# Loop over further expert rounds placed behind the last expert, router logits in one product, and tokens placed ahead of their weights in a two-layer diffusion transformer with a mixture of experts

## The chip, the cores and the metric

One Trainium2 chip, one of its cores. The metric is the device time in microseconds of one execution; lower is better. The engines are called TensorE (PE; its weight loads are listed as PEld), VectorE (DVE), ScalarE (ACT), GpSimd (POOL) and SyncE (SP). SyncE computes nothing here; it issues DMA transfers. GpSimd issues some as well, through its own software queue (q0 in the listings; SyncE's is q1).

## The reference, cut to what matters

256 latent tokens and 256 context tokens of width 1024 pass two layers. Layer 0 mixes them by attention, layer 1 by an S5 state-space scan. Each layer ends with a mixture of 32 experts in 4 groups, of which every token uses two. In layer 1 only the latent tokens are needed after the mixer.

```python
def hierarchical_moe(h, w_group, b_group, w_router, b_router, w_gate, w_up, w_down):
    t = h.reshape(-1, D_MODEL)
    g_logits = (t @ w_group + b_group)
    g_idx = jnp.argmax(g_logits, axis=-1)
    g_w = jnp.max(jax.nn.softmax(g_logits, axis=-1), axis=-1, keepdims=True)
    e_logits = (t @ w_router + b_router).reshape(-1, MOE_GROUPS, MOE_EXPERTS_PER_GROUP)
    e_logits = jnp.einsum('tg,tge->te', one_hot(g_idx, MOE_GROUPS), e_logits)
    e_w, e_idx = lax.top_k(jax.nn.softmax(e_logits, axis=-1), MOE_TOP_K)
    e_w = e_w / jnp.sum(e_w, axis=-1, keepdims=True)
    expert = g_idx[:, None] * MOE_EXPERTS_PER_GROUP + e_idx
    combine = jnp.einsum('tk,tke->te', g_w * e_w, one_hot(expert, MOE_EXPERTS))
    for e in range(MOE_EXPERTS):
        hid = jax.nn.silu(t @ w_gate[e]) * (t @ w_up[e])
        y = y + combine[:, e:e + 1] * (hid @ w_down[e])
```

## The kernel before

The kernel is written against a tile framework with a manual schedule: the order of instructions on each engine is the order of the Python code, and generators (`prep`, `open`, `quad`, `turned` and others) are advanced by hand with `next` to interleave them. The program is straight-line code except for one loop, in `overflow`, which stands twice, once for each layer.

An expert holds 64 slots (`W`). A token's place in an expert is its rank among the tokens that chose it. If an expert has more than 64 tokens, further rounds are needed; `count` (L736) computes the number of rounds into `rounds`, and `overflow` (L1022) loads it into a register of every engine (L1026), copies the places (L1028, L1029) and runs a `For_i` loop (L1030) from round 1 to that number. With the inputs of this case there is one round, so the loop body runs zero times.

Layer 0 has four tiles of 128 tokens (`nt` = 4), layer 1 two. For each tile `prep` (L597) normalises the tokens, transposes them on TensorE (L626), forms the router logits (L633, a copy L636, a second product L647 with a selector, and the bias at L649), and `route` (L653) chooses the group and the two experts with some thirty small VectorE instructions, forms the ranks (L689) and the weights (L697 to L706). `place` (L710) builds a one-hot of the slot (L717) and, with a product (L718), writes the token number and its weight into the slot table `acc` in PSUM. The last tile advances `opening`, which contains `count`.

`experts` (L937) begins with `slots` (L720), which copies `acc` to SBUF, and then differs by layer:

- Layer 0 (`direct`): `pairs` (L728, four copies on GpSimd) and `indices` (L811) form row numbers, three `gather`s (L824, issued on GpSimd) fetch the token rows of experts 0 to 5 from a DRAM copy `td`, GpSimd issues the weights of expert 2, `overflow` stands, and `turned` (L828) transposes the first gathered rows (L835).
- Layer 1: `overflow` stands, then `pairs` and the one-hots for the next four experts. Rows are selected by products (`take`, L761) with split copies `parts` of the tokens (L642 on ScalarE, L643 on GpSimd).

Then 32 experts follow. For each, `hidden` (L841) does the gate and up products (L848), `down` (L864) the second product (L869) of the expert before. Every second expert, `places` and `split` scale the results (L897, L898; in layer 1's last pair L891), and `combine` (L907) adds them back to the tokens with products (L913). The last pair is combined in `last`, which in layer 0 also issues the first S5 loads (`s5.load(7)`, in the order v0 v1 v2 w0 k0 w1 v3; two more, w2 and v4, follow at the scan's first step) and in layer 1 the output transfers (L1903).

Weights are fetched by SyncE, three transfers of 1 MB for an expert, into a ring of slots: 11 in layer 0, 16 in layer 1. SyncE issues a transfer when the slot's last reader is done, and takes its instructions in order. Ahead of `experts`, layer 0 fetches two experts (`ahead(2)`), layer 1 five.

## Time and profile before

| | us |
|---|---|
| median of 3 runs | 1153.84 |
| lowest and highest | 1153.43, 1157.52 |
| the profiled execution, its own time | 1157.44 |
| its span, first to last instruction | 1155.7 |
| mean granted TensorE clock, of 2.4 GHz | 0.942 |
| TensorE busy | 987.2 (85%) |
| VectorE busy | 730.1 (63%) |
| ScalarE busy | 324.6 (28%) |
| GpSimd busy | 139.9 (12%) |

Times of instructions below are from the span's start. The first layer's experts begin at 403 us and end at about 720; the S5 scan runs from there to about 845; the second layer's experts run from 882 to the end. A granted clock of 0.50 is the lower of TensorE's two levels (1.2 GHz), 1.00 the upper one.

### The profile page before, as it was taken

What the parts mean: (1) busy time and instruction counts of PE and PEld (TensorE: products, weight loads), DVE (VectorE), ACT (ScalarE), POOL (GpSimd) and SP (SyncE); (2) the same over time, 40 slices, a digit from 0 to 9 for tenths busy, and PEclk for the clock granted to TensorE, in tenths of its full rate; (3) what the DMA queues carried; (4) which work ended last, traced back from release to release, by engine and by line L of the source; (5) the groups of instructions that cost most, each with busy time, mean ns of one, the idle gap of its engine ahead of it and who ended that gap; (6) DMA issues with size and microseconds to landing.
All of it is one profiled execution on the core that took longest, in us unless ns stands there. A gap on an engine that the chain in (4) does not pass through costs nothing. (4 is left out here: it accounts for less than half of the span.)

```text
span 1155.7 us, 17511 instructions
## 1 busy us (share of the span) xinstructions
PE 987.2 (85%) x6627; PEld 552.9 (48%) x6627; DVE 730.1 (63%) x1804; ACT 324.6 (28%) x704; POOL 139.9 (12%) x206
## 2 busy tenths in 40 slices
PE   2798889879998199999988977678977999999997
PEld 0443444444444055555544532365755555555553
DVE  7779888993445214455788987399974444534444
ACT  3422334343111032121221212693531211221210
POOL 2311121123111100000000002011421000000000
PEclk9899999989999589999998988889987999999999
DMA  9954854855994889999885886399975999999951
GB/s 298 353 178 137 287 197 151 276 198 174 386 407 143 332 317 409 385 403 354 329 333 205 321 323 158 90 227 327 393 283 232 355 382 383 377 378 380 384 200 37
DMA packets 88232, 331.75 MB, mean 287 GB/s; under 512 B 10040, under 2 KB 18968, under 8 KB 69712
## 3 DMA queue, kind: packets, MB, share of 16 engines
q1 hardware_dynamic: 68736, 290.05, 68.3%
q10 hardware_dynamic: 11424, 21.12, 5.2%
q0 software_dynamic: 7984, 19.42, 5.0%
q8 instruction: 54, 0.88, 0.3%
q14 instruction: 34, 0.28, 0.1%
HBM read 313.76 MB, written 20.99 MB: 290 GB/s over the span
## 5 line engine op out<-in xcount | busy, mean ns | idle before, releaser
L848 PE MATMUL gu<-ring,xq 128*64 128x256 f32 x1056 | 147.1, 394 | 4.6 <-DVE sl L853 2.3
L848 PE MATMUL gu<-more,xq 128*64 128x256 f32 x992 | 135.9, 386 | 0.0
L848 PEld LDWEIGHTS gu<-ring,xq 128*64 128x64 f32 x1056 | 83.3, 142 | 63.5 <-issue 28.4
L913 PE MATMUL co<-yh,oT 128*128 128x512 f32 x188 | 87.9, 468 | 24.6 <-DVE z L904 9.1
L848 PEld LDWEIGHTS gu<-more,xq 128*64 128x64 f32 x992 | 77.0, 138 | 53.4 <-issue 23.3
L352 PE MATMUL acc<-ring,uT 128*128 128x512 f32 x192 | 91.7, 609 | 2.9 <-ACT uT L328 2.9
L852 ACT ACTIVATE sl<-gu 64x256 f32<-64x256 f32 x64 | 24.1, 377 | 247.0 <-PE gu L848 247.0
L921 DVE TENSOR_TENSOR sum<-sum,co 128x512 f32<-128x512 f32 x92 | 59.5, 682 | 33.6 <-PE co L913 33.5
L913 PE MATMUL co<-yl,oT 128*128 128x512 f32 x188 | 78.4, 417 | 0.6 <-DVE yl L898 0.6
L853 DVE TENSOR_TENSOR sl<-gu,sl 64x256 f32<-64x256 f32 x64 | 27.3, 426 | 79.4 <-ACT sl L852 78.2
L861 DVE COPY hT<-ht 128x128 f32<-128x128 f32 x64 | 18.4, 287 | 87.5 <-PE ht L859 87.4
L869 PE MATMUL y<-ring,hT 128*64 128x512 f32 x272 | 68.8, 628 | 0.4 <-DVE hT L861 0.4
L913 PEld LDWEIGHTS co<-yh,oT 128*128 128x128 f32 x188 | 35.8, 191 | 59.1 <-issue 18.2
L869 PE MATMUL y<-more,hT 128*64 128x512 f32 x240 | 58.0, 604 | 0.4 <-DVE hT L861 0.4
L352 PEld LDWEIGHTS acc<-ring,uT 128*128 128x128 f32 x192 | 34.4, 193 | 36.5 <-issue 32.5
L142 PE MATMUL gv<-ring,cT 128*32 128x256 f32 x512 | 34.6, 412 | 18.0 <-DMA ring<-mod_w 18.0
L915 DVE TENSOR_TENSOR h<-h,co 128x512 f32<-128x512 f32 x64 | 41.1, 681 | 5.7 <-PE co L913 5.7
L821 POOL DMA_INDIRECT xg<-td,row x16 | 16.1, 1006 | 208.1 <-PE xt L835 206.3
L913 PEld LDWEIGHTS co<-yl,oT 128*128 128x128 f32 x188 | 36.5, 194 | 8.5 <-DVE yl L898 5.4
L835 PE MATMUL xt<-ident,xg 128*128 128x128 f32 x128 | 22.0, 300 | 20.6 <-issue 19.9
L407 ACT ACTIVATE pr<-sc,mx 128x256 f32<-128x256 f32 (+1 forms) x32 | 18.6, 580 | 74.5 <-DVE mx L406 74.5
L898 DVE SCALAR_TENSOR_TENSOR yl<-z,pt,yh 128x512 fp32r<-128x512 f32 x30 | 22.5, 751 | 25.8 <-ACT yh L897 25.8
(434 smaller groups left out, 1856.7 us busy)
## 6 DMA issues: line engine op xcount, KB each, us to landing
ring<-moe_w_down SPq DMA_DIRECT2D x34, 1024.0 KB, 9.8
ring<-moe_w_gate SPq DMA_DIRECT2D x33, 1024.0 KB, 7.6
ring<-moe_w_up SPq DMA_DIRECT2D x33, 1024.0 KB, 8.3
ring<-mod_w SPq DMA_DIRECT2D x32, 1024.0 KB, 8.5
more<-moe_w_gate SPq DMA_DIRECT2D x30, 1024.0 KB, 7.4
more<-moe_w_up SPq DMA_DIRECT2D x30, 1024.0 KB, 9.2
more<-moe_w_down SPq DMA_DIRECT2D x29, 1024.0 KB, 11.2
more<-mod_w SPq DMA_DIRECT2D x16, 1024.0 KB, 15.5
```

The lines of the kernel that those rows point to most:

```text
L142: nc.tensor.matmul(self.bank[i, b][32 * q:32 * q + 32, o:o + 256], self.cT[:, k, :], self.tiles[i, ch, k // 2][:, k % 2, 256 * q:256 * q + ...
L352: nc.tensor.matmul(acc, uT[:, k, 128 * t:128 * t + 128], wq[b][k // 4][:, k % 4, :], start=(k == 0), stop=(k == KT - 1))
L407: nc.scalar.activation(pr[:, 0:nk], s[:, 0:nk], AF.Exp, bias=mx[:, h, 0:1], accum_out=mx[:, h, 1:2])
L835: nc.tensor.transpose(p[:, 128 * i:128 * i + 128], self.xg[:, k % 3, 4 * b + i::KT], self.c.ident)
L848: nc.tensor.matmul(p[s:s + 64, 0:HID], xT[k], w[k // 4][:, k % 4, :], start=(k == 0), stop=(k == KT - 1), skip_group_check=True)
L852: nc.scalar.activation(sl, p[0:64, 0:HID], AF.Silu)
L853: nc.vector.tensor_tensor(sl, p[64:128, 0:HID], sl, op=OP.mult)
L869: self.c.nc.tensor.matmul(p[o:o + 64, :], hT[:, f, :], wd[f][:, 512 * n:512 * n + 512], start=(f == 0), stop=(f == 1), skip_group_check=True)
L898: nc.vector.scalar_tensor_tensor(lo, y, w, hi.bitcast(F32), op0=OP.mult, op1=OP.subtract)
L913: nc.tensor.matmul(p, oh[:, 128 * n:128 * n + 128], y, start=(i == 0), stop=(i + 1 == len(rows)))
L915: nc.vector.tensor_tensor(h, h, p, op=OP.add)
L921: nc.vector.tensor_tensor(a, a, p, op=OP.add)
```

## The change

- `overflow` leaves the head of `experts` and is called at the end of the loop over experts, behind the `split` of the last pair and ahead of `last`. In its body one tile is replaced by a part of another.
- The logits are one product: the transposed tokens are the weights, the router's 40 columns move. The copy, the selector product and one step of the generator go; the bias is added from PSUM.
- In `route`, the negated maxima and the three exponentials move behind the choice of experts. The token numbers are placed first, in columns 0 to 31 of `acc`, the weights later, in columns 32 to 63, with the same one-hots.
- In layer 0 a new `start`, called by the last tile's `route` between the two placings, computes the row numbers from `acc` directly and issues the three gathers and expert 2's weights. `pairs` and `slots` run after the opening.
- In layer 1 the subtraction on GpSimd is cut in four, and the order in which the two tiles' steps are advanced is a new string, `LAST`.

```diff
--- before.py
+++ after.py
@@ -629,24 +629,18 @@
         yield
         p = self.bank("gu")
         for k in range(KT):
-            g = 64 * (k % 2)
-            nc.tensor.matmul(p[g:g + 64, 0:128], self.wr[:, k, :], tT[:, k, :], start=(k < 2), stop=(k >= KT - 2),
-                             skip_group_check=True)
-        lg = wk.tile([128, 128], F32, name="lg", tag="A", bufs=2)
-        nc.vector.tensor_copy(lg, p[:, 0:128])
+            nc.tensor.matmul(p[:, 0:40], tT[:, k, :], self.wr[:, k, 0:40], start=(k == 0), stop=(k == KT - 1))
+        L = wk.tile([128, 40], F32, name="L", tag="L", bufs=2)
+        nc.vector.tensor_add(L, p[:, 0:40], self.br)
         if self.xg is None:
             hi, lo = self.part.get(n) or self.part_tiles(n)
 
             x = t.rearrange("p (q k) -> p k q", k=KT)
             hi, lo = (y.rearrange("p (k q) -> p k q", k=KT) for y in (hi, lo))
             nc.scalar.activation(hi, x, AF.Copy)
-            nc.gpsimd.tensor_tensor(lo, x, hi.bitcast(F32), op=OP.subtract)
+            for k in range(0, KT, 2):
+                nc.gpsimd.tensor_tensor(lo[:, k:k + 2], x[:, k:k + 2], hi[:, k:k + 2].bitcast(F32), op=OP.subtract)
             self.parts.append((hi, lo))
-        yield
-        p = self.bank("xt")
-        nc.tensor.matmul(p[:, 0:40], lg, c.sel40, start=True, stop=True)
-        L = wk.tile([128, 40], F32, name="L", tag="L", bufs=2)
-        nc.vector.tensor_add(L, p[:, 0:40], self.br)
         yield
         yield from self.route(n, L)
 
@@ -666,22 +660,22 @@
 
         V.max(gm, L[:, 0:8])
         V.max_index(gk, gm, L[:, 0:8])
-        V.tensor_scalar(ngm, gm[:, 0:1], -1.0, None, op0=OP.mult)
         V.tensor_copy(gi, gk[:, 0:1])
         V.tensor_scalar(g1, self.token[:, 0:4], gi, -BIG, op0=OP.not_equal, op1=OP.mult)
-        A.activation(gx, L[:, 0:4], AF.Exp, bias=ngm, accum_out=gs)
         V.tensor_tensor(xe.rearrange("p (g e) -> p g e", g=4), L[:, 8:40].rearrange("p (g e) -> p g e", g=4),
                         g1[:, :, None].to_broadcast([128, 4, 8]), op=OP.add)
         V.max(em, xe)
         V.max_index(ek, em, xe)
-        V.tensor_scalar(nm, em[:, 0:1], -1.0, None, op0=OP.mult)
         V.tensor_copy(ei, ek[:, 0:2])
-        A.activation(ex, xe, AF.Exp, bias=nm, accum_out=es)
-        A.activation(m, em[:, 0:2], AF.Exp, bias=nm)
         oh = self.oh[:, n]
         V.tensor_tensor(oh, self.token[:, None, 0:32].to_broadcast([128, 2, 32]), ei[:, :, None].to_broadcast([128, 2, 32]),
                         op=OP.is_equal)
         V.tensor_tensor(self.ob[:, n], oh[:, 0], oh[:, 1], op=OP.add)
+        V.tensor_scalar(ngm, gm[:, 0:1], -1.0, None, op0=OP.mult)
+        V.tensor_scalar(nm, em[:, 0:1], -1.0, None, op0=OP.mult)
+        A.activation(gx, L[:, 0:4], AF.Exp, bias=ngm, accum_out=gs)
+        A.activation(ex, xe, AF.Exp, bias=nm, accum_out=es)
+        A.activation(m, em[:, 0:2], AF.Exp, bias=nm)
         yield
         yield
         p = self.bank("gu")[:, 0:32]
@@ -694,28 +688,37 @@
             for _ in range(self.nt - self.opened):
                 next(self.opening)
         V.tensor_reduce(self.pe[:, n], x, axis=AX.X, op=OP.add)
+        rhs = self.rhs[:, n]
+        for k in range(2):
+            V.tensor_scalar(rhs[:, k, 0:32], oh[:, k], self.tok[:, n:n + 1], None, op0=OP.mult)
+        hots = self.place(n, self.pe[:, n], [rhs[:, k, 0:32] for k in range(2)], slice(0, 32))
+        if self.xg is not None and n + 1 == self.nt:
+            self.start()
+        if self.one:
+            yield
         V.reciprocal(gw, gs)
         V.reciprocal(es, es)
         V.tensor_scalar(m, m, es, None, op0=OP.mult)
         V.tensor_tensor(den, m[:, 0:1], m[:, 1:2], op=OP.add)
         V.reciprocal(den, den)
         V.tensor_scalar(m, m, den, gw, op0=OP.mult, op1=OP.mult)
-        rhs = self.rhs[:, n]
         for k in range(2):
-            V.tensor_scalar(rhs[:, k, 0:32], oh[:, k], self.tok[:, n:n + 1], None, op0=OP.mult)
             V.tensor_scalar(rhs[:, k, 32:64], oh[:, k], m[:, k:k + 1], None, op0=OP.mult)
-        yield
-        self.place(n, self.pe[:, n], [self.rhs[:, n, k] for k in range(2)])
-
-    def place(self, n, pe, rhs):
+        self.place(n, self.pe[:, n], [rhs[:, k, 32:64] for k in range(2)], slice(32, 64), hots)
+
+    def place(self, n, pe, rhs, s, hots=None):
 
         nc, V = self.c.nc, self.c.nc.vector
-        if n == 0:
+        if n == 0 and s.start == 0:
             self.acc = self.bank("ht")
+        if hots is None:
+            hots = [self.wk.tile([128, 128], F32, name="A", tag="A", bufs=4 if self.one else 2) for k in range(2)]
+            for k in range(2):
+                V.tensor_scalar(hots[k], self.slot, pe[:, k:k + 1], None, op0=OP.is_equal)
         for k in range(2):
-            A = self.wk.tile([128, 128], F32, name="A", tag="A", bufs=2)
-            V.tensor_scalar(A, self.slot, pe[:, k:k + 1], None, op0=OP.is_equal)
-            nc.tensor.matmul(self.acc[:, 0:64], A, rhs[k], start=(n + k == 0), stop=(n == self.nt - 1 and k == 1))
+            nc.tensor.matmul(self.acc[:, s], hots[k], rhs[k], start=(n + k == 0 and s.start == 0),
+                             stop=(n == self.nt - 1 and k == 1), skip_group_check=True)
+        return hots
 
     def slots(self, name=""):
 
@@ -763,6 +766,16 @@
         for i, x in enumerate(self.parts[n]):
             self.c.nc.tensor.matmul(p, x[:, k, :], g, start=(n + i == 0 and first), stop=(n + 1 == self.nt and i == 1),
                                     skip_group_check=True)
+
+    def start(self):
+
+        self.indices()
+        for k in range(3):
+            self.gather(k)
+        c = self.c
+        c.queue = c.nc.gpsimd
+        self.first[2] = self.weights(2)
+        c.queue = c.nc.sync
 
     def open(self):
 
@@ -811,11 +824,13 @@
 
     def indices(self):
 
-        V, x = self.c.nc.vector, self.pt[:, 0, 0]
+        V = self.c.nc.vector
         f = self.wk.tile([128, 16], F32, name="rowf")
         self.row = self.wk.tile([128, 16], U32, name="row")
-        V.tensor_scalar(f, x, 0.0, FAR, op0=OP.is_lt, op1=OP.mult)
-        V.tensor_tensor(self.row, f, x, op=OP.add)
+        for r, v in ((slice(0, 64), 0), (slice(64, 128), 1)):
+            x = self.acc[r, v:32:2]
+            V.tensor_scalar(f[r], x, 0.0, FAR, op0=OP.is_equal, op1=OP.mult)
+            V.scalar_tensor_tensor(self.row[r], x, -1.0, f[r], op0=OP.add, op1=OP.add)
 
     def rows_to(self, out, row):
         self.c.nc.gpsimd.indirect_dma_start(out, None, self.td[:, :], bass.IndirectOffsetOnAxis(ap=row, axis=0),
@@ -938,23 +953,13 @@
 
         c = self.c
         wt = self.first
-        ts = self.slots()
         direct = self.xg is not None
-        if direct:
-            self.pairs(ts)
-            self.indices()
-            for k in range(3):
-                self.gather(k)
-            c.queue = c.nc.gpsimd
-            wt[2] = self.weights(2)
-            c.queue = c.nc.sync
-        self.overflow()
         if direct:
             self.sum, self.sums = [self.row_tile("sum", "r") for _ in range(self.nt)], 10
             for _ in self.turned(0):
                 pass
         else:
-            self.pairs(ts)
+            self.pairs(self.slots())
             g = [self.onehot_tile("r") for _ in range(2)]
             ahead = self.quad(1, g[1])
             next(ahead)
@@ -1003,6 +1008,8 @@
                         pass
                     oh = self.places(e // 2 - 1)
                     parts = self.split(e // 2 - 1, p, oh, e == NE)
+                    if e == NE:
+                        self.overflow()
                     if e < NE:
                         pieces = (self.combine(n, j, f, parts, k) for k in [e // 2 - 1] for f in range(2) for n, j in tiles)
             if e > 14:
@@ -1031,7 +1038,7 @@
             for x in (pe, pos):
                 V.tensor_scalar(x, x, -float(W), None, op0=OP.add)
             for t in range(self.nt):
-                self.place(t, pe[:, t], [self.rhs[:, t, k] for k in range(2)])
+                self.place(t, pe[:, t], [self.rhs[:, t, k] for k in range(2)], slice(0, 64))
             ts = self.slots("o")
             with c.tc.For_i(0, NE, 1) as e:
                 at = wk.tile([128, self.nt, 1], F32, name="oat")
@@ -1069,7 +1076,7 @@
                     pass
                 p = self.bank("y0")
                 self.down(self.turn_hidden(self.hid), wd, [(p, 0), (p, 64)])
-                y = wk.tile([128, 512], F32, name="oy", tag="yh0")
+                y = ov[:, 512:1024]
                 nc.scalar.activation(y, p, AF.Copy, scale=sw)
                 for t, (n_, j) in enumerate(self.tiles_j):
                     sel = wk.tile([128, 128], F32, name="osel", tag="sl", bufs=2)
@@ -1090,6 +1097,9 @@
     def row_tile(self, name, tag="t4"):
         return self.wk.tile([128, D], F32, name=name, tag=tag, bufs=2 if self.one and tag == "r" else T4)
 
+
+
+LAST = "1001111100112"
 
 TWO_PI = 2.0 * math.pi
 C1 = 6.28125
@@ -1811,6 +1821,7 @@
                     next(beside, None)
             for _ in moe.opening:
                 pass
+            moe.pairs(moe.slots())
             s5 = S5(c, par)
             st = c.small.tile([128, 4, 2], F32, name="s5st", bufs=1)
 
@@ -1885,12 +1896,12 @@
             more = right.enter_context(tc.tile_pool(name="more3", bufs=1, reuse_waits="tile"))
             c.use(*c.order(), *[(more, f"more{i}") for i in range(10)])
             moe.ahead(5)
-            for n in map(int, "101101110111"):
-                next(prep[n], None)
-            for _ in prep[0]:
-                pass
-            next(moe.opening)
-            for _ in chain(prep[1], moe.opening):
+            for n in map(int, LAST):
+                if n == 2:
+                    next(moe.opening)
+                else:
+                    next(prep[n], None)
+            for _ in chain(*prep, moe.opening):
                 pass
             lat = a["out"][0].rearrange("(b i) d -> i b d", i=8)
 
```

## Rows read from the trace of the kernel before

**Rows 1.** Stages: length, busy PE, PEld, DVE, ACT, POOL (instructions), clock, DMA share, GB/s.
```profile
375.00:403.00 28.00, 2.23 (x16) 1.77 (x14) 6.65 (x41) 1.24 (x6) 5.74 (x10) 0.50 0.86 343
450.00:500.00 50.00, 50.00 (x323) 28.69 (x320) 25.39 (x48) 9.37 (x18) 2.93 (x3) 1.00 1.00 394
```

**Rows 2.** Waits of SyncE's queue, 375 to 410 us: in total, times, longest.
```profile
SPq L1030 <- DMA more<-moe_w_down: 10.0, 1, 10.0
SPq L1026 <- DVE sc L698: 8.3, 1, 8.3
```

**Rows 3.** Order of time, first layer's last tile: start, us, instruction, count, idle before.
```profile
373.27 1.81 PE L633 MATMUL gu<-tT,wr 128*64 128x128 f32 x16 [0.69 <-ACT tT L98]
...
376.39 0.17 DVE L667 MAX8 gm<-L 128x8 f32<-128x8 f32 x1
...
380.12 0.15 DVE L750 CAST rounds<-rf 128x1 int32<-128x1 f32 x1
...
382.41 0.93 PEld L718 LDWEIGHTS ht<-rhs,A 128*128 128x128 f32 x4 [3.44 <-DVE A L717]
...
385.83 1.14 POOL L821 DMA_INDIRECT xg<-td,row  x1 [1.14 <-issue]
...
403.44 1.12 PE L835 MATMUL xt<-ident,xg 128*128 128x128 f32 x4 [19.91 <-issue]
```

**Rows 4.** First gather, issue to landing (last number); then all sixteen gathers.
```profile
xg<-td,row POOLq DMA_INDIRECT x1, 4.8
...
DMA to landing us min/median/max: 3.3/5.1/8.3
```

**Rows 5.** Order of time, second layer's start.
```profile
866.80 2.74 DVE L700 TENSOR_TENSOR sc<-sc 128x1 f32<-128x1 f32 x1
...
875.30 0.19 PE L689 MATMUL gu<-ob,ones 128*128 128x32 bf16 x1
...
880.96 0.18 DVE L1029 COPY pos_r<-pos 128x64 f32<-128x64 f32 x1
...
882.33 5.21 PE L848 MATMUL gu<-ring,xq 128*64 128x256 f32 x32 [2.24 <-POOL pt L734]
```

**Rows 6.** Slot waits, 404 to 690; expert 2's products, 406 to 420; queues' packets, 486 to 488.
```profile
SPq L89 <- PE y L869: 222.8, 28, 13.0
...
L848 PE MATMUL gu<-more,xq x4: 379/379/379, 419.7 to 419.9; 128*64 128x256 f32 x4
...
q1 hardware_dynamic: 90, 0.54, 66.0%
q0 software_dynamic: 100, 0.23, 32.3%
```

**Rows 7.** Order of time, first layer's end and the scan's first product.
```profile
684.93 0.33 SPq L89 DMA_DIRECT2D ring<-s5v  x1
...
708.45 1.41 DVE L898 SCALAR_TENSOR_TENSOR yl<-y,pt,yh 128x512 fp32r<-128x512 f32 x2 [1.96 <-ACT yh L897]
...
709.79 0.69 DVE L904 TENSOR_TENSOR z<-co,gate 128x512 f32<-128x512 f32 x1
...
741.45 0.37 PE L1562 MATMUL vp<-un,ring 128*64 128x64 f32 x1
```

**Rows 8.** Order of time, second layer's end.
```profile
1146.18 1.41 DVE L891 SCALAR_TENSOR_TENSOR yw<-y,pt,gate 128x512 f32<-128x512 f32 x2 [1.50 <-PE y L869]
1146.98 3.89 PE L913 MATMUL co<-yw,oT 128*128 128x512 f32 x8 [0.84 <-DVE yw L891]
```

**Rows 9.** Single microseconds of the second layer's start, columns as in rows 1.
```profile
881.00:882.00 1.00, 0.00 (x0) 0.00 (x0) 0.14 (x2) 0.50 (x1) 0.39 (x3) 1.00 0.07 16
882.00:883.00 1.00, 0.67 (x4) 0.48 (x6) 0.00 (x0) 0.79 (x1) 0.33 (x2) 0.54 0.68 98
...
885.00:886.00 1.00, 1.00 (x10) 0.66 (x8) 0.00 (x0) 0.00 (x0) 0.00 (x0) 0.76 0.56 229
```

## The prediction

> **What bounds the kernel now.** I read the busy time by stage first. Between 375 and 403 us TensorE works 2.23 of 28 us, while inside the first layer's expert stage it works 50.00 of 50 us at full clock [rows 1]. So the expert stage is TensorE's, and the 28 us ahead of it are somebody's wait. The waits of SyncE's queue say whose: at the loop over further rounds (L1030) it waited 10.0 us for the landing of expert 2's down weights, and at L1026 it had stood 8.3 us until the round count was there [rows 2]. The order of time gives the rest [rows 3]: the gathers of token rows start at 385.83, the first product on gathered rows (L835) at 403.44. A gather lands 4.8 us after its start, here at 390.6 [rows 4]. TensorE could have begun about 390.9 and began 12.5 us later, because entering the loop drains every transfer in flight, three of them megabyte loads of an expert that is needed much later. The second layer has the same loop at 881, with nothing in flight: its last copy ends at 881.14, TensorE goes on at 882.33 [rows 5]. That 1.19 us is the bare price of passing the loop.
>
> Is the expert stage really TensorE's and not the DMA's? Its DMA share is 1.00 at 394 GB/s [rows 1], so this is close. But SyncE waited for TensorE to free a slot 28 times, 222.8 us in all [rows 6]; weights are ahead, and a stage that starts earlier should end earlier by as much.
>
> **First layer, start of the experts (the gain).** The logits product now has token columns as weights: 16 loads of 128x128 instead of 128x64. At the lower clock level such a load takes 0.93/4 = 0.23 us (L718) [rows 3], so 16 take 3.7, the addition about 0.25: 3.95 us, where the old way took 376.39 - 373.27 = 3.1 us with its copy and second product [rows 3]. Loss 0.8; at the upper level the loads halve, a gain of 0.9. I take the loss, since L718 ran in the same poorly filled stretch. From the first MAX8 (376.39) to the first one-hot being ready (weight load at 382.41) VectorE does 32 small steps in 6.0 us, 0.19 each. Ten of them (two negations, six of the weights, two of their one-hots) now come later: gain 1.9. From that weight load to the gather, 3.4 us, the four copies on GpSimd fall away and two index steps more come in on VectorE: gain about 0.5. The loop is gone. The gather starts 0.8 - 1.9 - 0.5 = 1.6 us earlier, at 384.2; lands at 389.0 if it takes 4.8 again [rows 4]; TensorE starts at 389.2 instead of 403.44. **Gain 14.2 us.** All gathers of the run took 3.3 to 8.3 us [rows 4], so this term reaches from 10.7 to 16.6 with the clock's 1.7 added.
>
> Three things move with it. SyncE, no longer held at L1026, issues expert 3's gate and up weights (2.1 MB; their slots were read by products that stand ahead in TensorE's order) 8.3 us before the count was stored at 380.1, about 372 [rows 2, 3], ahead of gathers and of expert 2's weights, which go through GpSimd's queue. Do expert 2's weights come too late? They are needed when the old trace began on them, 419.7 - 403.44 = 16.3 us after the start [rows 3, 6]: at 405.5. In mid-stage with both queues loaded, GpSimd's queue moved 100 packets (0.23 MB) beside 90 of SyncE's (0.54 MB) in 2 us [rows 6]: packets share evenly, bytes don't, since gathered rows travel in small packets. A gather of 0.26 MB (half of its slots hold a token) takes 2.3 us at that 115 GB/s, so 2.5 of its 4.8 us pass before bytes move: from 386.7 three gathers last until 393.7. From there expert 2's packets are as large as SyncE's, and even if SyncE always has more to send, half of 394 GB/s brings the gate and up weights (2.1 MB) in by 404.4. That is 1.1 us in time; I charge 0.5. At a third of the bytes throughout it would be 409.8: a stall of 4.3 us.
> The Trainium skill (DMA: Bandwidth & Descriptors, "Queues, rings and completion order") says that each DMA engine takes turns between queues packet by packet; 100 against 90 agrees, and it speaks against this change, since whatever SyncE issues early takes every second turn from the gathers. By it alone expert 2 is in time, as above.
> The copies to pairs now run on GpSimd behind gathers and weight issues; their first reader is the placement at expert 2, some 15 us later: nothing. The other three tiles' logits run beside the attention's output: 0 to 1 us, taken as 0.
> Net for this place: **-13.7**.
>
> **First layer, end of the experts (the first price).** The loop now stands behind the split of expert 31. VectorE ends the split at 708.45 + 1.41 = 709.86 [rows 7]; it adds two copies (0.4), then the loop's 1.19 [rows 5]: TensorE's combination starts at 711.45, and its two products (0.49 each at the upper level [rows 8]) let VectorE's first scaling, now at 709.79, start at 712.4: +2.6. At the lower level +3.6. I take **+3.0**. In flight at that point is nothing: the S5 weights, which SyncE used to issue at 684.93 as slots came free [rows 7], are issued in the code behind the loop and so stand queued behind it now. Nine pieces (v0 v1 v2 w0 k0 w1 v3 w2 v4, about 9.4 MB) leave from 711 on; at 394 GB/s they are in by 735, and the scan's first product, old at 741.45 [rows 7], needs only v0. Cost 0 on this reading; its failure is the last rival.
>
> **Second layer, start.** Loop and copies vanish from the way of expert 0: 882.33 - 880.96 = 1.4, nearly certain [rows 5]. GpSimd's subtraction, now cut in four, held VectorE 2.74 us on a one-column step; but tile 1's logits now stand on TensorE behind tile 0's placing product and before the opening products, whose end released the step at 875.30 [rows 5]. So of the 2.6 won I count 0.5 (bounds 0 and 2.6). Expert 0's first 32 products took 5.21 us, part of it at the lower level after TensorE's pause [rows 5, 9]; a shorter pause returns 0 to 1.3, I take 0.8. The DMA is idle then (share 0.07 at 881 [rows 9]): no weights were missing. **-2.7**, bounds -1.4 and -5.3.
>
> **Second layer, end (the second price).** Nothing follows to hide it. The first combination started at 1146.98, behind the first of two scaled rows; now both (to 1147.59 [rows 8]), the two copies (0.3) and the loop (1.19) go first: 1149.1, +2.1. TensorE then has been idle for 3 us. In the second layer's start the granted clock was full at 881 to 882 with TensorE idle, 0.54 in the next microsecond and 0.76 at 885 [rows 9]: some 3 us at half rate, in which a product chain of 3.89 us [rows 8] loses 1.5. **+3.6**, bounds 2.1 (no fall) and 6.0 (slow throughout).
> The Trainium skill (Runtime: NRT & Kernel Launch, "Instruction fetch mechanics") states that a taken branch out of the fetched window stalls the engine for a fetch. It speaks against two loops on the path's end; the old trace's 1.19 us contains whatever this cost there, and in the sum nothing is added for it.
>
> **Sum.** -13.7 + 3.0 - 2.7 + 3.6 = -9.8. The profiled execution took 1157.44 us (span 1155.7, 1.7 around it) and would take 1147.6. It lies 3.6 above the median of the three timed runs, 1153.84; the terms are stretches of the program, so I take them from the median as well: **1144.0 us**.
>
> **Rivals.**
> (a) The early SyncE loads hurt more: a gather at its slowest (+3.5) and expert 2 late by 2 to 4. For it: DMA share 1.00. Against: the share counted in packets. Gain some 4 to 5 us instead of 10: about 1149.
> (b) Clock kinder and GpSimd's hold worth all of it: ends +2.6 and +2.1, second start -5.3: 1153.84 - 13.7 + 4.7 - 5.3 = 1139.5.
> (c) The expert stage is DMA-paced. Then starting TensorE earlier wins only idle DMA time: 0.14 of 28 us is 3.9 [rows 1], with as much again in the first refills (an estimate) 8, and -8 + 3.0 - 2.7 + 3.6 gives 1149.7. Against it: the 222.8 us of waiting for slots.
> (d) Slower: the S5 scan starves. Its place is the first steps from 741; its cause, the 9.4 MB that all leave behind the loop. They may take until about 744 at no cost, which needs 285 GB/s. To end 5.8 us slower than before, they must eat the gain too, 15.6 us late: 9.4 MB in 49 us, under 195 GB/s. Then 1160. Against it: v0 to v2 go first and 394 GB/s is what large pieces reach [rows 1]; for it, k0 goes in eight small ones.
>
> **How the numbers follow.** About 0.5% (5.8 us) is what a measurement here tells from no change. Forecast 0.52, all of it faster; (b) 0.20, faster; (a) 0.18, a third of it faster; (c) 0.06, same; (d) 0.04. So faster 0.78, same 0.18, slower 0.04. Below 1137 all terms would have to stand at their kind ends; above 1150 lie (d) and half of (a). Range 1137 to 1150.
>
> **What would show it.** Right: L835 first at about 389, with the wait of SyncE at L1030 gone there; SyncE's expert 3 loads near 372; expert 2's products about 16 us after the start with no gap; the distance from the first expert product to the last one unchanged; two loops of 1.2 to 2 us behind L898 and L891. Wrong: a gather landing after 392, TensorE waiting for weights of expert 2, a DMA wait inside either new loop, a late v or w piece in the scan, a last combination ending over 5 us behind its old distance.

## The result

The changed kernel took 1170.24 us (median; 1162.29 to 1171.91) beside 1155.49 us of the kernel before on the same chip: a ratio of 1.0111, interval 1.0065 to 1.0156. Run again later (e10_again, below) the ratio was 1.0049 (1.0012 to 1.0086). It is slower both times; the forecast was 1144.0 with a range up to 1150. The profiled execution is the shortest of the five of the first comparison, 1162.29 us (span 1160.3) at a mean granted clock of 0.951; the other four took 1166.7 to 1171.9 us at 0.944 down to 0.931. The medians are 14.8 us apart, the spans of the two profiled executions only 4.6: the profile shows the mechanism in the mildest of these executions, and what the longer ones add lies in no profile.

Laid out by marks that both kernels have (the start of the first and of the last product of a line), the two spans divide like this, in us:

| stretch | before | after | difference | predicted |
|---|---|---|---|---|
| start to the first attention output product (L445) | 278.8 | 280.7 | +1.9 | 0 |
| first to last attention output product | 86.7 | 102.1 | **+15.4** | **0** |
| to the first turned block of the experts (L835, now L850) | 37.9 | 25.0 | -12.9 | -13.7 |
| to the first layer's last expert product (L848, now L863) | 294.6 | 292.2 | -2.4 | 0 |
| to the scan's first product (L1562, now L1572) | 43.5 | 43.7 | +0.2 | +3.0 |
| to the second layer's opening products (L764, now L767) | 130.3 | 133.4 | +3.1 | 0 |
| to its first expert product | 10.5 | 8.9 | -1.6 | -1.9 |
| to its last expert product | 259.2 | 257.4 | -1.8 | -0.8 |
| to the end of the span | 14.2 | 16.9 | +2.7 | +3.6 |
| sum | 1155.7 | 1160.3 | +4.6 | -9.8 |

The -2.7 that was forecast for the second layer's start is divided here: 0.8 of it, expert 0's first products, lies behind the mark.

The gain that was forecast came. It was eaten in a stretch ahead of it for which the prediction had written 0. The lines of the attention output's products, before and then after (durations min/median/max in ns, first and last start):

```profile
L445 PE MATMUL oa<-ring,oT x64: 592/592/697, 278.8 to 344.7; 128*128 128x512 f32 x64
L445 PE MATMUL acc<-ring,oT x64: 592/592/697, 294.6 to 365.5; 128*128 128x512 f32 x64
```
```profile
L445 PE MATMUL oa<-ring,oT x64: 592/592/1201, 280.7 to 360.7; 128*128 128x512 f32 x64
L445 PE MATMUL acc<-ring,oT x64: 592/592/1201, 296.5 to 382.8; 128*128 128x512 f32 x64
```

The same 128 passes; after, some take twice as long. TensorE's waits in this stretch, before (two rows), then after (three): in total, times, longest.

```profile
PE ht L718 <- DVE A L717: 1.7, 1, 1.7
PE gu L689 <- DVE ob L684: 0.6, 2, 0.3
```
```profile
PE ht L719 <- DVE A L717: 3.5, 3, 1.2
PE ht L719 <- DVE rhs L706: 2.6, 3, 1.0
PE gu L683 <- DVE ob L673: 2.4, 2, 1.2
```

The order of time of the changed kernel shows how one tile's routing step makes these waits:

```profile
314.69 1.98 PE L445 MATMUL acc<-ring,oT 128*128 128x512 f32 x4
...
317.89 0.18 PE L683 MATMUL gu<-ob,before 128*128 128x32 bf16 x1 [1.22 <-DVE ob L673]
...
319.22 0.63 PE L719 MATMUL ht<-rhs,A 128*128 128x32 f32 x4 [1.16 <-DVE A L717]
...
320.88 1.06 PE L719 MATMUL ht<-rhs,A 128*128 128x32 f32 x4 [1.02 <-DVE rhs L706]
...
321.75 3.76 PE L445 MATMUL acc<-ring,oT 128*128 128x512 f32 x4
```

Rank product (L683), the products that place the token numbers and those that place the weights (both L719) now follow each other in TensorE's queue, each behind a chain of VectorE steps, with no attention output product between. The kernel before yielded ahead of its placing, so L445 and L142 stood there, and the placing (L718) began without a wait:

```profile
315.55 0.19 PE L689 MATMUL gu<-ob,before 128*128 128x32 bf16 x1 [0.30 <-DVE ob L684]
315.59 1.10 PE L445 MATMUL acc<-ring,oT 128*128 128x512 f32 x2
...
318.49 0.66 PE L718 MATMUL ht<-rhs,A 128*128 128x64 f32 x4
```

After the change the attention output's products were ready the whole time; they stood behind the waiting ones. After three waits of 1.0 to 1.2 us the four L445 passes at 321.75 take 3.76 us where four took 1.98 at 314.69. Windows of 2 us (length, busy PE, PEld, DVE, ACT, POOL, then clock, DMA share, GB/s):

```profile
318.00:320.00 2.00, 0.70 (x5) 0.52 (x4) 1.72 (x11) 1.43 (x7) 0.00 (x0) 1.00 1.04 410
320.00:322.00 2.00, 1.12 (x5) 1.12 (x6) 0.86 (x5) 0.00 (x0) 0.00 (x0) 0.70 1.03 406
322.00:324.00 2.00, 2.00 (x3) 0.90 (x4) 0.00 (x0) 0.00 (x0) 1.69 (x3) 0.50 1.02 408
324.00:326.00 2.00, 2.00 (x10) 0.33 (x12) 0.00 (x0) 0.00 (x0) 0.00 (x0) 0.50 0.90 352
```

The granted clock goes from 1.00 to its lower level, 0.50, inside the step and stays there into the window from 326 to 328 (0.59); it does so once more behind tile 1's step (350 to 360). Tile 2's step has two such waits, not three, and no fall. In the kernel before it is 1.00 in every window from 278 to 366.

The +15.4 by busy and idle time of the lines: waits 8.5 against 2.3 (+6.2); L445 63.8 against 60.5 and L142, its neighbour, 21.2 against 20.1 (+4.4, the clock); placing 5.1 against 2.0 (+3.1: 24 passes instead of 12, some at half clock); logits 5.6 against 4.4 (+1.2). Sum 14.9; the other 0.5 isn't laid to a line.

The place that the prediction was about, first layer's last tile, after (answers to [rows 3]):

```profile
390.58 1.98 PE L632 MATMUL gu<-wr,tT 128*128 128x40 f32 x16 [0.69 <-ACT tT L98]
...
392.83 0.17 DVE L661 MAX8 gm<-L 128x8 f32<-128x8 f32 x1
...
397.38 0.93 PEld L719 LDWEIGHTS ht<-rhs,A 128*128 128x128 f32 x4 [1.98 <-DVE A L717]
...
399.56 1.15 POOL L836 DMA_INDIRECT xg<-td,row  x1 [9.38 <-DVE sc L700]
...
407.75 1.11 PE L850 MATMUL xt<-ident,xg 128*128 128x128 f32 x4 [5.69 <-DMA xg<-td,row]
```

From the first MAX8 to the gather it is 6.7 us instead of 9.4, from the gather to the first turned block 8.2 instead of 17.6.

### The profile page after: what moved, and what is told of

It reads as the page before. It is cut to its first block, busy times and chain, and to the rows that moved or that the text cites. A ratio compares the mean times of both kernels' runs of the same rounds, so it can differ in the third digit from the quotient of the medians.

```text
span 1160.3 us, 17551 instructions
## 1 busy us (share of the span) xinstructions
PE 993.9 (86%) x6639; PEld 561.9 (48%) x6639; DVE 729.3 (63%) x1800; ACT 322.9 (28%) x703; POOL 140.6 (12%) x212
## 5 line engine op out<-in xcount | busy, mean ns | idle before, releaser
L863 PE MATMUL gu<-ring,xq 128*64 128x256 f32 x1056 | 144.3, 388 | 2.7 <-DVE sl L868 2.6
L863 PE MATMUL gu<-more,xq 128*64 128x256 f32 x992 | 136.0, 386 | 0.8 <-DVE sl L868 0.8
L863 PEld LDWEIGHTS gu<-ring,xq 128*64 128x64 f32 x1056 | 81.3, 139 | 60.2 <-issue 23.9
L863 PEld LDWEIGHTS gu<-more,xq 128*64 128x64 f32 x992 | 76.9, 138 | 54.4 <-issue 22.9
L876 DVE COPY hT<-ht 128x128 f32<-128x128 f32 x64 | 18.4, 287 | 87.0 <-PE ht L874 86.8
L142 PE MATMUL gv<-ring,cT 128*32 128x256 f32 x512 | 35.6, 421 | 18.2 <-DMA ring<-mod_w 18.2
L912 ACT ACTIVATE yh<-z,pt 128x512 fp32r<-128x512 f32 x30 | 21.6, 722 | 55.9 <-DVE z L919 55.9
```

The source lines that it names most:

```text
L142: nc.tensor.matmul(self.bank[i, b][32 * q:32 * q + 32, o:o + 256], self.cT[:, k, :], self.tiles[i, ch, k // 2][:, k % 2, 256 * q:256 * q + ...
L863: nc.tensor.matmul(p[s:s + 64, 0:HID], xT[k], w[k // 4][:, k % 4, :], start=(k == 0), stop=(k == KT - 1), skip_group_check=True)
L912: nc.scalar.activation(hi, y, AF.Copy, scale=w)
```

## The experiments

Theory A: in the merged steps of tiles 0 to 2 TensorE waits for VectorE in its own queue, and loses the clock. Theory B: the one-product logits slow the attention output. Theory C: the moved loops and early loads cost the time.

All ratios are to the kernel before, run beside the experiment; "profiled" means the marks of the table above.

**e1_steps.** The changed kernel, for tiles 0 to 2 of the first layer:

```diff
+        if not self.one and n + 1 < self.nt:
+            yield
         hots = self.place(n, ..., slice(0, 32))
-        if self.one:
+        if self.one or n + 1 < self.nt:
             yield
```

> The changed kernel with two yields put back for tiles 0 to 2 of the first layer (one ahead of the token products, one ahead of the gate weights), so that again an attention output product stands in TensorE's queue between the rank product, the token products and the weight products. Theory A (TensorE stands in its own queue behind VectorE's chain in these merged steps and then loses the clock): first to last attention output product goes from 102.1 us back to 86 to 90, the granted clock stays at 1.00 there, and the whole comes to 1144 to 1150 us, 12 to 18 under the profiled run of the changed kernel and faster than the kernel before. Theory B (the logits in one product, with its 128-column loads and 40-column products, slows that stretch): it stays at 98 or more and the whole at 1157 or more. Theory C (the loops at the ends and the early weight loads cost the time): the stretch may mend, but the whole stays at 1154 or more.

Measured: 1151.87 us, ratio 0.9957 (0.9934 to 0.9980). The attention output took 90.8 us with the clock at 1.00 all through. TensorE's waits there:

```profile
PE gu L683 <- DVE ob L673: 1.2, 1, 1.2
PE gu L683 <- DVE sc L674: 1.2, 1, 1.2
PE ht L721 <- DVE A L719: 0.6, 3, 0.2
```

Two yields turn slower into faster: the mechanism is A. But 90.8 is above the expected 86 to 90, and the median 2 us above; a second cost is left, which e4 and e7 look for.

**e2_loop.** The kernel before with the loops moved (and the one tile in the loop's body replaced, as in the change) and nothing else:

```diff
-        self.overflow()
...
                     parts = self.split(e // 2 - 1, p, oh, e == NE)
+                    if e == NE:
+                        self.overflow()
```

> The kernel before with one edit: the loop over further rounds stands behind the last expert in both layers; logits, placing and gathers as before. Theory A: the attention output keeps its 86.7 us; the start of the first layer's experts gains 3 to 7 us (the loop's wait for DMAs goes, the gathers still start where they did), the second layer's start gains 0 to 2, the two ends lose 1 to 6 together: 1148 to 1156 us. Theory C (loops at the ends cost what the change lost): 1160 or more.

Measured: 1144.01 us, 0.9882 (0.9846 to 0.9919), better than expected. In its profile (span 1140.6) the first layer's start takes 29.4 us (-8.5), the second's 8.5 (-2.0), its expert stage 255.7 (-3.5), the end 15.8 (+1.6). C falls: the moved loops are a gain, and alone they bring 12.0 us in the medians, more than the 9.8 that the prediction gave to the whole change.

**e3_onestep.** The kernel before with that one yield taken out:

```diff
-        yield
+        if self.one or n + 1 == self.nt:
+            yield
         self.place(n, self.pe[:, n], ...)
```

> The kernel before with one edit: for tiles 0 to 2 of the first layer the yield between the rank product and the placing is gone, so rank, gates, one-hots and placing come in one step with no attention output product between. Theory A: the attention output's 86.7 us grow by 6 to 16, with the granted clock falling below 1.00 inside it, and the whole comes to 1161 to 1171 us. Theory B (it was the logits product): no change, 1153 to 1157.

Measured: 1169.57 us, 1.0100 (1.0070 to 1.0130). This one yield costs the kernel before as much as the whole change did. In the profiled run, the shortest of its seven, the attention output takes 94.8 us (+8.1), with one fall of the clock behind one tile's step:

```profile
PE ht L719 <- DVE A L718: 7.9, 3, 2.6
PE gu L689 <- DVE ob L684: 0.6, 2, 0.3
```
```profile
316.00:318.00 2.00, 0.19 (x1) 0.10 (x1) 1.47 (x11) 0.62 (x3) 0.00 (x0) 1.00 1.03 408
318.00:320.00 2.00, 1.13 (x6) 0.74 (x6) 1.01 (x7) 0.00 (x0) 0.52 (x1) 0.93 1.04 414
320.00:322.00 2.00, 2.00 (x14) 0.56 (x16) 0.00 (x0) 0.00 (x0) 1.17 (x2) 0.50 1.02 401
```

**e4_logits.** The kernel before with the logits in one product:

```diff
-            nc.tensor.matmul(p[g:g + 64, 0:128], self.wr[:, k, :], tT[:, k, :], ...)
-        lg = ...; nc.vector.tensor_copy(lg, p[:, 0:128])
+            nc.tensor.matmul(p[:, 0:40], tT[:, k, :], self.wr[:, k, 0:40], ...)
...
-        nc.tensor.matmul(p[:, 0:40], lg, c.sel40, start=True, stop=True)
```

> The kernel before with one edit: the router logits in one product of eight accumulating matmuls of 40 columns, the selection product and VectorE's copy left out, the yields kept in number. Theory A: the attention output stays within 1.5 us of 86.7 and the whole within 1152 to 1157 us. Theory B: the attention output grows by 6 or more and the whole to 1161 or more.

Measured: 1159.14 us, 1.0022 (0.9996 to 1.0048): between the two expectations, and not told from no change. The attention output takes 87.8 us (+1.1). That small part is real: three tiles' logits, in the kernel before and in this one:

```profile
L633 PE MATMUL gu<-tT,wr 128*64 128x128 f32 x48 | 3.3, 279 | 0.0
...
L647 PE MATMUL xt<-sel,lg 128*128 128x40 f32 x6 | 1.1, 274 | 0.0
```
```profile
L632 PE MATMUL gu<-wr,tT 128*128 128x40 f32 x48 | 5.6, 277 | 0.0
```

A product fewer, yet 5.6 us of TensorE instead of 4.4: in these traces a pass with 128-column weights starts 0.11 us after the one before it, though only 40 columns move, and two of those with 64-column weights start in that time. B is right in sign and far too small to be the cause. The rest of this kernel's +3 in the median isn't explained: its profile has +4.0 between the scan and the second layer, a stretch in which e1_steps, with the same logits, has 0.

**e5_lastplace.** e2_loop, and in the first layer's last tile alone the tokens placed first, the row numbers read from PSUM, and gathers and expert 2's loads issued there:

```diff
+        direct = self.xg is not None and n + 1 == self.nt
+        if direct:
+            ...
+            hots = self.place(n, self.pe[:, n], [rhs[:, k, 0:32] for k in range(2)], slice(0, 32))
+            self.start()
         V.reciprocal(gw, gs)
```

> e2_loop (the kernel before with the loops behind the last experts) with a second part of the change: in the first layer's last tile alone the token halves are placed first, the row numbers are read from PSUM and the gathers and expert 2's loads are issued right there. Logits in two steps, tiles 0 to 2 and the second layer as in the kernel before. Theory A: the time from the last attention output product to the first turned block of the experts falls from the 29.4 us of e2_loop to 24.5 to 27 (the changed kernel has 25.0), and the whole comes to 1138 to 1142 us against 1144 of e2_loop. Theory B (the early gathers bring nothing once the loop is gone, since the weight loads stand ahead of them): 28.5 or more, and the whole 1143 or more.

Measured: 1140.97 us, 0.9850 (0.9809 to 0.9890); once more as e12_best 1143.64. The first layer's start takes 24.7 us (24.8 in e12_best) against 29.4: -4.7, as A said. In the medians 1141.0 and 1143.6 can't be told from e2_loop's 1144.0.

**e6_loop0.** e2_loop with the second layer's loop put back ahead of its experts:

```diff
+        if self.one:
+            self.overflow()
...
-                    if e == NE:
+                    if e == NE and not self.one:
                         self.overflow()
```

> e2_loop with the second layer's loop put back ahead of its experts; the first layer's stays behind the last expert. Theory A (the loop at the second layer's end costs about what it gives at its start): the start of the second layer's experts is 2 us later, the end 1.5 to 3 us shorter, the whole 1142 to 1146 us, the same as e2_loop within 2. Theory C (moving the second layer's loop behind the experts was a loss): 1140 or less. If it was a gain: 1147 or more.

Measured: 1148.74 us, 0.9924 (0.9896 to 0.9953): the third case, moving this loop too was a gain. The profiles differ by 6.3 us: 2.2 in the start of the program, ahead of all that differs; start of the second experts 10.6 against 8.5; their stage 259.3 against 255.7; end 14.1 against 15.8; net 4.0 for the loop. The medians' ratios overlap a little, but the stage takes about 259.2 us in every profile with this loop ahead of the experts (before, e3_onestep, e4_logits) and 255.6 or 255.7 in e5_lastplace, e8_third and e12_best, which have it behind them. The 3.6 in the stage had no term in this expectation (0.8 in the prediction). It goes with the granted clock: TensorE is busy 251.0 us in the stage against 247.7. Expert 0's first 32 products and a window near the end of the stage, in e6_loop0 and in e2_loop:

```profile
873.47 5.36 PE L848 MATMUL gu<-ring,xq 128*64 128x256 f32 x32 [2.19 <-POOL pt L734]
1127.00:1130.00 3.00, 3.00 (x16) 1.47 (x12) 1.95 (x3) 0.00 (x0) 0.00 (x0) 0.50 0.00 0
```
```profile
869.13 3.67 PE L848 MATMUL gu<-ring,xq 128*64 128x256 f32 x32
1122.00:1125.00 3.00, 3.00 (x22) 1.80 (x22) 2.03 (x4) 0.00 (x0) 0.00 (x0) 1.00 0.00 0
```

With the loop ahead, TensorE waits 2.19 us before expert 0 and the clock is at 0.50 from 874 to 877; with the loop behind there is no such wait and the clock stays up. What makes the difference near the end isn't shown: the waits ahead of it are the same in both. SyncE, too, stood still in e6_loop0 (waits between 840 and 902):

```profile
SPq L1029 <- DVE sc L698: 18.4, 1, 18.4
```

Its queue stands at the loop's count for 18.4 us, the loads of the next experts behind it. That this delays a weight isn't shown: no wait of TensorE in the stage names a load.

**e7_twostep.** e1_steps with the first layer's logits in two steps again:

```diff
+        if self.one:
+            (the one product)
+        else:
+            (the eight products, the copy)
+            yield
+            nc.tensor.matmul(p[:, 0:40], lg, c.sel40, start=True, stop=True)
```

> e1_steps (the changed kernel with its yields put back) with one edit: in the first layer the logits come in two steps as before (64-column weight loads, copy, selection product). Theory A with the logits as a second, smaller cost: the attention output falls from 90.8 us to 86.5 to 88.5 and the whole from 1152 to 1141 to 1147 us. If the logits product is harmless in either form: 1150 to 1154.

Measured: 1146.11 us, 0.9881 (0.9840 to 0.9922); the attention output takes 86.1 us (expected 86.5 to 88.5). From 90.8 to 86.1, more than the product's own 1.2: with the logits' yield back, most of the 2.4 us of waiting at the rank product is gone too (0.6 left).

**e8_third.** e5_lastplace with expert 3's loads on GpSimd behind the gathers:

```diff
-        self.first[2] = self.weights(2)
+        for e in (2, 3):
+            self.first[e] = self.weights(e)
```

> e5_lastplace with one edit: expert 3's loads are issued on GpSimd behind the gathers and expert 2's loads, where SyncE issued them ahead of the gathers. Theory A with contention (loads queued ahead of the gathers stretch their landing from the 4.5 us of the kernel before to 8.8 to 9.5): the gathers land in 4.5 to 6.5 us, the experts start 2 to 4 us earlier than in e5_lastplace, and the whole comes out 1 to 4 us under it. Rival (the gathers are slow for another reason, or expert 3 then comes late): landing stays at 8 or more, or the whole is the same or longer.

Measured: 1140.53 us, 0.9857 (0.9805 to 0.9910): the same. The gathers (issue to landing, median of three) in the kernel before, in e5_lastplace and in e8_third:

```profile
xg<-td,row POOLq DMA_INDIRECT x3, 4.5
```
```profile
xg<-td,row POOLq DMA_INDIRECT x3, 9.4
```
```profile
xg<-td,row POOLq DMA_INDIRECT x3, 7.2
```

So loads issued ahead do stretch the gathers, and expert 3's are a part of it; experts 0 and 1's are still arriving (the last of them lands at 393.8, the first gather at 393.0). But from the first gather to the first turned block it is 7.7 us against 8.1: the first gather gained 0.4, and that is what counts. The first layer's start takes 25.5 us against 24.7, no less. The rival stands for the time.

**e9_fill.** The changed kernel with useless work: ahead of each of the three waiting products of tiles 0 to 2,

```diff
+                q = self.bank("xt")
+                for _ in range(2):
+                    nc.tensor.matmul(q, c.ident, self.wr.rearrange("p k n -> p (k n)"), start=True, stop=True)
```

> The changed kernel with useless work added: in the first layer's tiles 0 to 2, ahead of the rank product, the token products and the weight products, two products of 128x512 each whose result nobody reads (18 in all, 36 passes of 0.59 us or 21 us of TensorE's time at the upper clock). They stand where TensorE waited for VectorE; they hide no useful work behind the waits. Theory A, the part of it that says the short waits cost less than the clock they trip: the granted clock stays at 1.00 from 280 to 370 us, the attention output takes 94 to 108 us, so no more than 6 above the changed kernel's 102.1 in spite of 21 us of added work, and the whole comes to 1158 to 1168 us in the profiled run. Rival (the waits alone cost the 15 us and the clock follows them at no price): the attention output takes 112 us or more and the whole 1172 or more.

Measured: 1160.68 us, 1.0042 (1.0006 to 1.0079), beside 1163.26 of e10_again. The attention output takes 102.1 us, as without the 36 added passes. The windows that stood at 0.50 above:

```profile
320.00:322.00 2.00, 2.00 (x9) 1.14 (x8) 1.60 (x10) 0.00 (x0) 0.00 (x0) 1.00 1.02 398
322.00:324.00 2.00, 2.00 (x9) 1.19 (x8) 0.00 (x0) 0.00 (x0) 1.17 (x3) 1.00 1.03 414
324.00:326.00 2.00, 2.00 (x19) 0.74 (x22) 0.00 (x0) 0.00 (x0) 0.52 (x1) 1.00 0.98 385
```

No wait of TensorE is left in the stretch and the clock never falls. The added passes take 17.5 us of busy time; the waits (8.5), the slow L445 and L142 passes (4.7) and the slow placing (1.9) give 15.1 back. Waits and clock together are worth about what the useless work costs; the idle time alone, 8.5 us, is about half of that.

**e10_again.** The changed kernel, unedited.

> The changed kernel once more, beside the filled one, for a second profile. Theory A: the clock falls once or more between 310 and 370 us, right after the merged steps of tile 0, 1 or 2, and the number of these falls goes with the time of the run: 1162 with two of them, about 4 us more for each further fall.

Measured: 1163.26 us (1155.43 to 1172.03), 1.0049 (1.0012 to 1.0086). The second profile (span 1157.9) has the same two falls, behind tile 0's step at about 322 and behind tile 1's at 352, and 102.1 us again. That longer executions hold more falls isn't shown: both profiles are of shorter ones.

**e11_second.** The changed kernel with the first layer's logits in two steps and tiles 0 to 2 placed whole in a step of their own; the loops, the last tile and all of the second layer's part stay.

```diff
+        whole = not self.one and n + 1 < self.nt
+        if not whole:
             hots = self.place(n, ..., slice(0, 32))
...
+        if whole:
+            yield
+            self.place(n, self.pe[:, n], [rhs[:, k] for k in range(2)], slice(0, 64))
```

> The changed kernel with the first layer's logits in two steps and its tiles 0 to 2 placed whole in a step of their own, as in the kernel before. What stays of the change: the loops behind the last experts, the first layer's last tile placed tokens first with the gathers right there, and all of the second layer's part (logits in one product, tokens first, the written-out order of steps). Theory A: the attention output comes back to 86.7 us within 1, and the whole to 1139 to 1144 us, the same as e5_lastplace within 2, since the second layer's part moves its start by no more than 1.5 us either way. If the second layer's part costs time: 1145 or more. If it gains: 1137 or less.

Measured: 1144.49 us, 0.9886 (0.9851 to 0.9921). The attention output is back at 86.7 us.

**e12_best.** e5_lastplace again.

> The kernel of e5_lastplace once more, beside e11_second on the same chip: 1138 to 1143 us, a ratio of 0.983 to 0.989 to the kernel before.

Measured: 1143.64 us, 0.9892 (0.9851 to 0.9932), the same as e11_second. So the second layer's part shows no gain: from the opening products to the first expert product e11_second takes 8.8 us, e12_best 8.6, e2_loop with the loop moved alone 8.5. The profiles even show a cost: from the scan's first product to the end of the span 413.3 or 413.4 us in e1_steps, e7_twostep, e10_again and e11_second, which have this part (so have e9_fill with 415.7 and the first profile of the changed kernel with 416.6), and 409.1 to 409.3 in e2_loop, e5_lastplace, e8_third and e12_best, which don't. Of the 4 us between the first four and the last four 1.5 lie in the expert stage and 1.1 in the end, where the granted clock falls in the first four before the last products are through and not in the last four. The medians of e11_second and e12_best (1144.5 and 1143.6) don't tell the two apart.

The version to keep is e2_loop or e5_lastplace, 1.1 to 1.5% under the kernel before; which of the two, these runs can't tell.

## Point by point

**The step that failed** is "The other three tiles' logits run beside the attention's output: 0 to 1 us, taken as 0", and with it the silence on what tokens first does to those tiles: the yield between rank and placing is gone in the first layer. "Beside" was taken as hidden. A prep step's products don't run beside the attention output, they stand between its products in one queue, and whatever they wait for, the output waits for: 102.1 us instead of 86.7, +15.4 where 0 to 1 was allowed, by 8.5 us of waits instead of 2.3 and a clock that fell twice. With a product between them again it is 90.8 (e1_steps) and, with the logits in two steps too, 86.1 and 86.7 (e7_twostep, e11_second). The Trainium skill says so of the queue (TensorE: Matmul & The Clock Gate, "The mechanism"): matmuls start and end in program order, without reordering. The rows agree: at 317.89, 319.22 and 320.88 TensorE waits with ready L445 products behind. No rival had this mechanism, so the range missed; rival (d), the only slower one, gave 1160 by another mechanism.

**First layer's start, -12.9 for -13.7:** right in sum, with two terms off. Logits 2.3 us to the first MAX8 instead of 3.1, a gain of 0.9 where 0.8 of loss was taken (the clock was still up for most of them). VectorE's and GpSimd's steps -2.7 for -2.4. Gather to first turned block -9.4 for -12.6: the gather's 4.8 us was mis-sized, it took 8.2, as slow as the slowest of [rows 4]. That is the piece of rival (a) that came true. The early loads stand in SyncE's queue at 389.56 and 393.14, ahead of the gather at 399.56, as predicted; e5_lastplace against e2_loop shows what the early issue itself is worth, about 4.7 us; the moved loop brings 8.5. By its own terms the upper end of the gain's range is 17.4 (14.2 + 1.5 + 1.7), not 16.6; nothing hangs on it.

**First layer's end, +0.2 for +3.0.** The price was there and was given back:

```profile
710.46 1.41 DVE L913 SCALAR_TENSOR_TENSOR yl<-y,pt,yh 128x512 fp32r<-128x512 f32 x2 [1.96 <-ACT yh L912]
...
711.86 0.22 DVE L1036 COPY pos_r<-pos 128x128 f32<-128x128 f32 x1
...
712.58 0.50 PE L928 MATMUL co<-yh,oT 128*128 128x512 f32 x1 [2.88 <-DVEq L1037]
...
714.13 0.69 DVE L919 TENSOR_TENSOR z<-co,gate 128x512 f32<-128x512 f32 x1 [2.06 <-PE co L928]
```

From the split to the first scaling 3.7 us instead of 1.3 [rows 7]: +2.3 for +2.6. But the scan's first product stands 43.7 us behind the last expert product, before 43.5; the same pair of numbers (late by 2.3, then level) is in all kernels with the moved loop. L1499 (now L1509) starts 22.4 us behind the last expert product, before 20.0, and its last pass starts 35.7 behind it, before 35.4: it runs at the upper clock level now, in the kernel before it began at the lower. The scan did not starve; rival (d) is out.

The loop's own price was mis-sized in both ends. From the end of its copies to TensorE's first product it is 0.5 us (712.08 to 712.58 here, 1149.66 to 1150.16 in the second layer, below), where 1.19 was taken as "the bare price". That figure was misread from the second layer's start in the kernel before:

```profile
881.57 0.76 POOL L734 COPY pt<-ts 64x32 f32<-64x32 f32 x4 [11.94 <-DVEq L1030]
```

GpSimd is past the loop at 881.57, 0.43 us behind the last copy. The other 0.76 are four copies that stand behind the loop, at whose end TensorE's row starts [rows 5].

**Second layer's start, -1.6 for -1.9, and its expert stage, -1.8 for -0.8.** Expert 0's first 32 products run at the upper clock now, -1.5 where 0.8 was taken [rows 5]:

```profile
886.04 3.67 PE L863 MATMUL gu<-ring,xq 128*64 128x256 f32 x32
```

e2_loop gets -2.0 and -3.5 without any of the second layer's other edits, so the 0.5 for GpSimd's cut subtraction and the rearranged steps wasn't there. "No weights were missing" was read from the idle DMA at 881 [rows 9]. The idle DMA doesn't show it, since with the loop at its old place SyncE's queue stood at the count for 18.4 us (e6_loop0) and could issue nothing; but TensorE's waits bear it out, as none in the stage names a load.

**Second layer's end, +2.7 for +3.6.** The gap and the fall of the clock both came, after:

```profile
1148.08 1.41 DVE L906 SCALAR_TENSOR_TENSOR yw<-y,pt,gate 128x512 f32<-128x512 f32 x2 [1.50 <-PE y L884]
...
1149.47 0.19 DVE L1036 COPY pos_r<-pos 128x64 f32<-128x64 f32 x1
...
1150.16 5.58 PE L928 MATMUL co<-yw,oT 128*128 128x512 f32 x8 [2.11 <-DVEq L1037]
```
```profile
1150.00:1152.00 2.00, 1.84 (x3) 0.81 (x4) 0.00 (x0) 0.00 (x0) 0.00 (x0) 0.56 0.02 4
```

First product 2.1 us behind the scaling instead of 0.8 [rows 8], +1.3 where +2.1 was taken (the loop's price again); eight passes in 5.58 us instead of 3.89, +1.7 where 1.5 was taken. In e2_loop the same gap leaves the clock at 1.00 and the passes at full rate:

```profile
1131.64 1.98 PE L913 MATMUL co<-yw,oT 128*128 128x512 f32 x4 [2.13 <-DVEq L1031]
```

**Not of the change as far as shown:** the +1.9 ahead of the attention output (280.0 in e5_lastplace and 278.4 in e12_best, one and the same kernel); the -2.4 in the first expert stage (e3_onestep and e4_logits, with the loop in its old place, have it too, and e12_best, with the loop moved, takes 294.6 as the kernel before); the +3.1 between scan and second layer (130.3 in e10_again, the same kernel as here). The second goes with the granted clock: 0.95 over that stage in the kernel before and in e12_best, 0.97 here and in e3_onestep. The third doesn't: 0.90 here, 0.89 in e10_again. What makes either differ from run to run was not followed up.

## What to carry to other kernels

Work that is interleaved into another loop's queue is free only while each of its steps waits for nothing. Before merging two steps, ask what stands in TensorE's queue between them, and whether that was what covered VectorE's latency; a yield that looks like bookkeeping may be worth 1%. When one place must get shorter, change that place alone: the last tile needed tokens first, the other three didn't.

## Not expected of the hardware

In tiles 0 and 1 three waits of 0.6 to 1.2 us within some 4 us were followed by six to seven us at the lower clock, the first time after more than 50 us at the upper one; behind tile 2's two waits of 1.0 and 1.2 us it stayed up. The Trainium skill describes such a case for gaps between groups of matmuls (TensorE: Matmul & The Clock Gate, "A second HAM failure mode: psum-queue depth-cycling"): short idle spells make the clock swing. By it the fall is no surprise; the page has no price, and e9_fill gives one here: 17.5 us of useless products in that stretch lost no time.

A gather issued behind megabytes of weight loads landed in 9.4 us instead of 4.5, and taking two megabytes out from ahead of it still left 7.2.
